# Expert layers of a two-block network on one core: both parts of x in one matmul from the first gate group on

## The chip, the core and the metric

One Trainium2 chip, one core. The time is device microseconds of one execution of the whole program. Three runs of the kernel before gave 3005.83, 3011.99 and 3014.3 us, median 3011.99.

## The reference

Two network blocks over 256 tokens of 1024 channels. The first has a convolution branch and a recurrent branch and then an expert layer; the second has two mixers, each followed by an expert layer. The change lies in the expert layer, which runs three times:

```
q = (x @ w_q) in 8 heads x 2 halves of 128;  s = q . sub_keys   (128 keys per half)
top 16 of each half, the 256 sums of pairs, top 16 of these:  expert e = i1*128 + i2
gate = softmax(the 16 best sums)                    # 128 experts per token, of 16384
act  = gelu(x . u[e]);   y = sum over the experts of gate * act * v[e]
```

## The kernel before

The kernel doesn't gather experts. It computes x . u for all 16384 experts and 256 tokens, multiplies by a dense matrix of gates that is zero almost everywhere, and multiplies that by v. A product in float32 precision is made of three matmuls: each operand is split into a high part (rounded, ScalarE, L82) and a low part (the rest, VectorE, L86), and high x high, high x low and low x high are added up.

An expert layer (`peer`) has these stages:

- Queries: 16 blocks of w_q, scores and, on VectorE, the top-16 searches.
- Up: 128 blocks of u (512 KB each, streamed by `stream`: SyncE's queue loads `raw`, four buffers; three buffers each of `hi` and `lo`). A block gives 128 experts x 256 tokens in a PSUM tile `pa`, on which ScalarE applies gelu into C (L1272, L1275).
- Down: 128 blocks of v. VectorE multiplies C by a gate tile (L1291), the result is split in two parts (L112, L113), and `acc_nat` (L168 to L170) adds up the output.

The gates of tokens 0 to 159 go through a table G in DRAM: GpSimd's indirect DMA adds them in (L1125, 128 + 32 adds a layer; `gts`, `idx` for the first 128 tokens, `pk` for the others). An add of a head waits until the adds of the head before on the same tokens have landed (`after`). At the start of the down stage GpSimd loads the first gate tile from G (L1286), behind all adds. The gates of tokens 160 to 255 are made in the core by `gates()`: 24 groups of four tokens, each with one-hot matrices B (VectorE, L1095) and A (two by VectorE, L1101, two by ScalarE, L1103 and L1104), four small matmuls (L1105), and a product into C (L1110) for the blocks done so far; for later blocks ScalarE copies the gates into C (L1109), and the block's activations are multiplied in (L1276).

The order comes from `pull`: before each block it advances the pending jobs (top-16 searches, the scatter of adds, then the spreading of picks and the groups of gates) by a budget, `rate` = 1.5, of which a group uses up 0.6 + 0.26 x 2 + 0.06 + 0.00416 x the number of blocks done. `behind` and `issue_after` keep VectorE's pieces in an order. An up block takes the form with three matmuls per 128 channels (`mm3`, 24 matmuls of 256 columns, L117 to L119) while jobs are pending, and after that the wide form: 8 matmuls of 512 columns with both parts of x (L1263), 8 of 256 columns with the low part of u (L1266), a copy (L1268) and a sum (L1270).

Of the kernel before, what the change touches and what calls it, by code (L numbers as in the profile page):

```python
# [40 lines left out]
class Net:  # L41
# [30 lines left out]
        nc.scalar.activation(warm, self.eps[RMS_EPS], AF.Sqrt)  # L72


    def stream(self, ap, n=1024):
        nc = self.nc
        raw = self.sp.tile([128, n], F32, tag="raw", name="raw", bufs=RAW)
        nc.sync.dma_start(raw, ap)
        self.chore(self.share)
        hi = self.sp.tile([128, n], F32R, tag="hi", name="hi")  # L80
        lo = self.sp.tile([128, n], F32R, tag="lo", name="lo")
        nc.scalar.copy(hi, raw)  # L82
        with self.behind():
            for i in range(0, n, 512):
                p = slice(i, min(i + 512, n))
                sub = nc.vector.tensor_tensor(lo[:, p], raw[:, p], hi[:, p].bitcast(F32), op=OP.subtract)  # L86
            self.los.append(sub)
        return hi, lo
# [966 lines left out]
    def peer(self, xh, xl, xx, wq, skT, uT, v, G, Gnext=None, rate=1.5, dve_a=2):  # L1055
# [9 lines left out]
        with ExitStack() as ctx:  # L1065
# [12 lines left out]
            cand = scr(256, 11008)  # L1078
            views = [self.topk_views(s_) for s_ in small]

            state = {"ub": 0, "tok": 256}
            SYNC = mybir.DependencyInfo(mybir.DependencyClass.Sync, mybir.DependencyReason.DATA)
            last, adds = [[], []], [[], []]

# [4 lines left out]
            def gates():  # L1089
                for t0 in range(252, TAB - 1, -4):  # L1090
                    t1 = t0 - 128
                    A = wp.tile([128, 4, 128], F32, tag="A", name="A")
                    B = wp.tile([128, 4, 128], F32, tag="B", name="B", bufs=TAIL)
                    pg = self.ps.tile([128, 4, 128], F32, tag="y", name="pg", bufs=4)
                    V.tensor_tensor(B, self.iota[:, None, :].to_broadcast([128, 4, 128]),  # L1095
                                    idT[:, 1, t1:t1 + 4, None].to_broadcast([128, 4, 128]), op=OP.is_equal)
                    for j in range(4):
                        t = t1 + j
                        i1, gg = idT[:, 0, t:t + 1], idT[:, 2, t:t + 1]
                        if j < dve_a:  # L1100
                            V.tensor_scalar(A[:, j], self.iota, i1, gg, op0=OP.is_equal, op1=OP.mult)  # L1101
                        else:
                            nc.scalar.activation(A[:, j], self.iota, AF.Abs, bias=idT[:, 3, t:t + 1])  # L1103
                            nc.scalar.activation(A[:, j], A[:, j], AF.Relu, scale=idT[:, 4, t:t + 1], bias=gg)  # L1104
                        nc.tensor.matmul(pg[:, j], B[:, j], A[:, j], start=True, stop=True)  # L1105
                    pT = pg.rearrange("p t b -> p b t")
                    n = state["ub"]
                    if n < 128:
                        nc.scalar.copy(C3[:, n:, t0:t0 + 4], pT[:, n:])  # L1109
                    V.tensor_tensor(C3[:, :n, t0:t0 + 4], C3[:, :n, t0:t0 + 4], pT[:, :n], op=OP.mult)  # L1110
                    state["tok"] = t0
                    yield 0.6 + 0.26 * dve_a + 0.06 + 0.00416 * n
# [59 lines left out]
                yield 1.8  # L1172

            def spread():
                pick = views[1]["pick"]
                pt = self.ps.tile([128, 512], F32, tag="y", name="pt", bufs=4)
                for i in range(3):
                    nc.tensor.transpose(pt[:, i * 128:i * 128 + 128], pick[:, i], self.ident)
                nc.scalar.copy(idT[:, 0:3].rearrange("p a b -> p (a b)"), pt[:, :384])
                V.tensor_scalar(idT[:, 3], idT[:, 0], -1.0, None, op0=OP.mult)  # L1180
                V.tensor_scalar(idT[:, 4], idT[:, 2], -1.0, None, op0=OP.mult)
                yield 1.0
                yield from gates()


            jobs = [[], []]
            for tt in range(2):
                for hf in range(2):
                    for g in range(8 * hf, 8 * hf + 8):
                        jobs[tt].append((g + 1, self.topk1(views[tt], S[tt], tmp, 2 * g + tt)))  # L1190
                    jobs[tt].append((8 * hf + 8, self.topk2(views[tt], cand, tmp, eq, 4 * hf)))
                    jobs[tt].append((8 * hf + 8, (scatter, scatter1)[tt](hf)))
            jobs[1].append((16, spread()))
            debt, now_ = [0.0], [None]

            def pull(budget, scored=16):


                debt[0] += budget
                with tc.issue_after(self.los[-PACE].ins):  # L1200
                    while debt[0] > 0:
                        if now_[0] is None:
                            q = next((q for q in jobs if q and q[0][0] <= scored), None)
                            if q is None:
                                debt[0] = 0.0
                                return
                            now_[0] = q.pop(0)[1]
                        c = next(now_[0], None)
                        if c is None:
                            now_[0] = None  # L1210
                        else:
                            debt[0] -= c
# [14 lines left out]
            for g in range(16):  # L1227
                hi, lo = self.stream(wq[g])
# [19 lines left out]
                self.clear(Gnext)  # L1248
                self.share = 0.35
            for b in range(128):  # L1250
                pull(rate)
                hi, lo = self.stream(uT[b])
                pa = self.ps.tile([128, 512], F32, tag="a", name="pu", bufs=4)
                src = pa
                if any(jobs) or now_[0]:
                    for c in range(8):
                        s = slice(c * 128, c * 128 + 128)
                        self.mm3(pa[:, :256], hi[:, s], lo[:, s], xh[:, c], xl[:, c], c == 0, c == 7)
                else:

                    for c in range(8):
                        s = slice(c * 128, c * 128 + 128)
                        nc.tensor.matmul(pa, hi[:, s], xx[:, c].rearrange("p x n -> p (x n)"), start=c == 0, stop=False)  # L1263
                    for c in range(8):
                        s = slice(c * 128, c * 128 + 128)
                        nc.tensor.matmul(pa[:, 256:], lo[:, s], xh[:, c], start=False, stop=c == 7)  # L1266
                    src = wp.tile([128, 256], F32, tag="sum", name="sum")
                    nc.scalar.copy(src, pa[:, 256:])  # L1268
                    with tc.issue_after(self.los[-1].ins):
                        V.tensor_tensor(src, src, pa[:, :256], op=OP.add)  # L1270
                tm = state["tok"]
                nc.scalar.activation(C3[:, b, :tm], src[:, :tm], AF.Gelu)  # L1272
                if tm < 256:
                    act = wp.tile([128, 256], F32, tag="act", name="act")
                    nc.scalar.activation(act[:, tm:], src[:, tm:256], AF.Gelu)  # L1275
                    V.tensor_tensor(C3[:, b, tm:], C3[:, b, tm:], act[:, tm:], op=OP.mult)  # L1276
                state["ub"] = b + 1
# [182 lines left out]
def build(nc, tc, a):  # L1460
    with ExitStack() as ctx:
# [16 lines left out]
        n.block1(a, *x[:2])  # L1478
        nc.gpsimd.dma_start(n.vec2, a["vec2"])
        py = peer(0, x)  # L1480
        x, y = xt(), xt()

        def first_a(fp):
            s = n.load_res(fp, hs[0])
            n.add_rms(fp, s, py, n.rows(fp, a["g_final_row"], "g"), *x[:2], norm=True)
            return s
        n.mixer_a(a, first_a, *x[:2], *y[:2], hs[1])
        py = peer(1, y)
        x, y = xt(), xt()

        def first_b(fp):
            s = n.load_res(fp, hs[1])
            n.add_ln(fp, s, py, a, (0, 1), *x[:2])
            return s
        n.mixer_b(a, first_b, *x[:2], *y[:2], hs[2])
        py = peer(2, y)
        with tc.tile_pool(name="fc", bufs=1) as fp:
            n.add_ln(fp, n.load_res(fp, hs[2]), py, a, (1, 1), dst=a["out"])
# [17 lines left out]
```

## Time and profile before

| | |
|---|---|
| profiled execution | 3022.11 us, span 3020.3 us, mean TensorE clock 0.986 |
| TensorE busy | 2929.5 us (97%) |
| VectorE busy | 2189.3 us (72%) |
| ScalarE busy | 1679.7 us (56%) |
| GpSimd busy | 947.0 us (31%) |
| L86, low parts | 1877 instructions, 1260.8 us, mean 684 ns |
| L1125, adds into G | 384 + 96 instructions, 699.7 + 150.4 us |
| matmuls of up blocks in the two forms | L117 to L119: 1656 each; L1263 and L1266: 1416 each |

Read it with the order in mind: up blocks use TensorE, VectorE and ScalarE while GpSimd's adds run beside them. The stage that follows needs both: the up blocks done and the adds landed. Three layers make every such row come three times. GpSimd's spans are rough, but their starts and the waits between them are not modelled.

### The profile page before, as it was taken

Reading aid. Unit: us, or ns where it says so; the run is one execution under the profiler, and the core shown is the slowest. Engines: PE = TensorE matmul, PEld = TensorE weight load, DVE = VectorE, ACT = ScalarE, POOL = GpSimd, SP = SyncE. Lnnn points to the kernel's source line nnn. Section 1 sums busy time; section 2 is a strip of 40 time slices with the busy share of each in tenths; the row PEclk is TensorE's granted clock in tenths of the full one; section 3 lists DMA queues with packets and bytes.
Section 4 is the critical chain, followed back from the end, with each engine's and each line's share of the span. In section 5 each row is a group of like instructions: output and inputs, shape, how many; then the busy total and the mean of one; then the engine's idle time right before and its main releaser. Section 6 shows DMA issues by size and latency. Waiting matters only on the chain.

```text
span 3020.3 us, 54408 instructions
## 1 busy us (share of the span) xinstructions
PE 2929.5 (97%) x19705; PEld 2620.8 (87%) x19705; DVE 2189.3 (72%) x5753; ACT 1679.7 (56%) x3054; POOL 947.0 (31%) x684
## 2 busy tenths in 40 slices
PE   9899999999999999999999999998999999999998
PEld 8888999987888888899998788887789998878886
DVE  6976998666666665799766666665589876666666
ACT  6345557765454454455866554445645676645543
POOL 0000387774000010058776200000008777510000
PEclk9999999999999998999999999999999999999999
DMA  9946676777677653477677676765347768767675
GB/s 310 322 128 201 175 183 161 160 190 181 224 221 225 224 191 106 151 190 188 141 179 191 188 222 225 226 219 175 108 153 194 171 145 190 189 197 223 223 225 185
DMA packets 253038, 581.46 MB, mean 193 GB/s; under 512 B 89392, under 2 KB 120384, under 8 KB 252512
## 3 DMA queue, kind: packets, MB, share of 16 engines
q1 hardware_dynamic: 172064, 535.60, 58.0%
q0 software_dynamic: 80704, 42.39, 9.2%
q8 instruction: 154, 2.52, 0.4%
q14 instruction: 116, 0.95, 0.1%
HBM read 539.78 MB, written 37.99 MB: 191 GB/s over the span
## 4 chain that ended last, share of the span: by engine, by line
PE 54%; POOL 9%; DMA 6%; issue 4%; DVE 3%; ACT 2%; POOLq 0%; DVEq 0%; SPq 0%; ACTq 0%
PE py L168 11%; PE py L170 11%; PE py L169 11%; POOL G L1125 8%; PE pu L118 3%; PE pu L117 3%; PE pu L119 3%; DMA G<-pk 3%; DMA G<-gts,idx 1%; PE pz L119 1%; PE pz L117 1%; PE pz L118 1%; DVE lo L86 1%; DMA res<-h 1%; DMA raw<-in_wq_dram 1%
## 5 line engine op out<-in xcount | busy, mean ns | idle before, releaser
L86 DVE TENSOR_TENSOR lo<-raw,hi 128x512 fp32r<-128x512 f32 (+1 forms) x1877 | 1260.8, 684 | 623.8 <-ACT hi L82 565.5
L82 ACT CAST hi<-raw 128x1024 fp32r<-128x1024 f32 (+1 forms) x939 | 980.8, 1046 | 946.0 <-issue 688.1
L1125 POOL DMA_INDIRECT G<-gts,idx x384 | 699.7, 1822 | 368.2 <-issue 133.2
L168 PE MATMUL py<-hi,cc 128*128 128x512 f32 x1536 | 600.4, 391 | 18.0 <-ACT cc L112 18.0
L170 PE MATMUL py<-hi,cc 128*128 128x512 f32 x1536 | 600.8, 391 | 0.0
L169 PE MATMUL py<-lo,cc 128*128 128x512 f32 x1536 | 600.2, 391 | 0.0
L117 PE MATMUL pu<-x,hi 128*128 128x256 f32 x1656 | 474.6, 287 | 0.0
L119 PE MATMUL pu<-x,lo 128*128 128x256 f32 x1656 | 468.7, 283 | 0.0
L118 PE MATMUL pu<-x,hi 128*128 128x256 f32 x1656 | 468.6, 283 | 0.0
L168 PEld LDWEIGHTS py<-hi,cc 128*128 128x128 f32 x1536 | 290.1, 189 | 79.7 <-ACT cc L112 19.6
L1263 PE MATMUL pu<-x,hi 128*128 128x512 f32 x1416 | 354.6, 392 | 0.0
L1286 POOL DMA_DIRECT2D gate<-G x96 | 51.9, 541 | 944.2 <-DVE C L1291 923.7
L170 PEld LDWEIGHTS py<-hi,cc 128*128 128x128 f32 x1536 | 289.7, 189 | 62.9 <-DVE cc L113 2.4
L169 PEld LDWEIGHTS py<-lo,cc 128*128 128x128 f32 x1536 | 290.0, 189 | 59.9
L118 PEld LDWEIGHTS pu<-x,hi 128*128 128x128 f32 x1656 | 317.6, 192 | 0.0
L117 PEld LDWEIGHTS pu<-x,hi 128*128 128x128 f32 x1656 | 317.4, 192 | 0.0
L119 PEld LDWEIGHTS pu<-x,lo 128*128 128x128 f32 x1656 | 317.3, 192 | 0.0
L1263 PEld LDWEIGHTS pu<-x,hi 128*128 128x128 f32 x1416 | 254.6, 189 | 45.5
L1266 PEld LDWEIGHTS pu<-x,lo 128*128 128x128 f32 x1416 | 193.2, 190 | 13.8
L1266 PE MATMUL pu<-x,lo 128*128 128x256 f32 x1416 | 197.4, 282 | 0.0
L1125 POOL DMA_INDIRECT G<-pk x96 | 150.4, 1567 | 99.6 <-DMA G<-pk 64.3
L112 ACT CAST cc<-C 128x256 fp32r<-128x256 f32 x384 | 153.0, 398 | 37.1 <-DVE C L1291 37.1
(497 smaller groups left out, 4325.1 us busy)
## 6 DMA issues: line engine op xcount, KB each, us to landing
raw<-in_u_dram SPq DMA_DIRECT2D x384, 512.0 KB
raw<-in_v_dram SPq DMA_DIRECT2D x384, 512.0 KB
G<-zero SPq DMA_DIRECT2D x120, 256.0 KB
gate<-G POOLq DMA_DIRECT2D x96, 320.0 KB
raw<-in_wq_dram SPq DMA_DIRECT2D x48, 512.0 KB
raw<-in_w_in_dram SPq DMA_DIRECT2D x38, 512.0 KB
raw<-in_a_w_inT_dram SPq DMA_DIRECT2D x14, 512.0 KB
raw<-in_b_wT_dram SPq DMA_DIRECT2D x14, 512.0 KB
```

The lines of the kernel that those rows point to most:

```text
L82: nc.scalar.copy(hi, raw)
L86: sub = nc.vector.tensor_tensor(lo[:, p], raw[:, p], hi[:, p].bitcast(F32), op=OP.subtract)
L112: nc.scalar.copy(hi, src)
L117: mm(out, lh, rh, start=start, stop=False)
L118: mm(out, lh, rl, start=False, stop=False)
L119: mm(out, ll, rh, start=False, stop=stop)
L168: mm(po[q], xh[:, ts], hi[:, h], start=f, stop=False)
L169: mm(po[q], xh[:, ts], lo[:, h], start=False, stop=False)
L170: mm(po[q], xl[:, ts], hi[:, h], start=False, stop=l)
L1125: i = nc.gpsimd.indirect_dma_start(G, bass.IndirectOffsetOnAxis(ap=ix, axis=0), g, None, compute_op=OP.add)
L1263: nc.tensor.matmul(pa, hi[:, s], xx[:, c].rearrange("p x n -> p (x n)"), start=c == 0, stop=False)
L1266: nc.tensor.matmul(pa[:, 256:], lo[:, s], xh[:, c], start=False, stop=c == 7)
```

## The change

From the moment at which the job that makes the gate groups starts (`spread`), a flag `wide` is set in this layer. From that block on, up blocks take the wide form, also while groups are pending; `pull` gets 0.55 per block instead of 1.5; and `stream` makes the low part of a u block in one VectorE instruction of 1024 columns instead of two of 512. Blocks before it, the down stage and all other streams are as they were.

```diff
-    def stream(self, ap, n=1024):
+    def stream(self, ap, n=1024, part=512):
...
-            for i in range(0, n, 512):
-                p = slice(i, min(i + 512, n))
+            for i in range(0, n, part):
+                p = slice(i, min(i + part, n))
                 sub = nc.vector.tensor_tensor(lo[:, p], raw[:, p], hi[:, p].bitcast(F32), op=OP.subtract)
...
-            state = {"ub": 0, "tok": 256}
+            state = {"ub": 0, "tok": 256, "wide": False}
...
             def spread():
+                state["wide"] = True
                 pick = views[1]["pick"]
...
-                pull(rate)
-                hi, lo = self.stream(uT[b])
+                pull(0.55 if state["wide"] else rate)
+                hi, lo = self.stream(uT[b], part=1024 if state["wide"] else 512)
...
-                if any(jobs) or now_[0]:
+                if not state["wide"]:
                     for c in range(8):
```

In the built program each layer has 69 blocks with three matmuls and 59 wide ones before, and 45 and 83 in the change. GpSimd's instructions stand in the same order in both. TensorE's order in the gate stretch, before: a group (`pg`) stands in front of nearly every block (the first matmuls of one are shown).

```order
L1105 MATMUL pg<-A,B 128x128 x4
L117 MATMUL pu<-x,hi 128x256
L118 MATMUL pu<-x,hi 128x256
L119 MATMUL pu<-x,lo 128x256
L117 MATMUL pu<-x,hi 128x256
```

In the change, the same place:

```order
L1105 MATMUL pg<-A,B 128x128 x4
L1264 MATMUL pu<-x,hi 128x512 x8
L1267 MATMUL pu<-x,lo 128x256 x8
L1264 MATMUL pu<-x,hi 128x512 x8
L1267 MATMUL pu<-x,lo 128x256 x8
L1264 MATMUL pu<-x,hi 128x512 x8
L1267 MATMUL pu<-x,lo 128x256 x8
L1105 MATMUL pg<-A,B 128x128 x4
```

Two or three wide blocks now stand between two groups. VectorE's order in the gate stretch, before (`lo` is a low part, B and A are a group's one-hot matrices, L1110 multiplies gates into C):

```order
L86 TENSOR_TENSOR lo<-raw,hi 128x512
L1110 TENSOR_TENSOR C<-C,pg 128x51x4
L86 TENSOR_TENSOR lo<-raw,hi 128x512
L1095 TENSOR_TENSOR B<-iota,idT 128x512
L1101 TENSOR_SCALAR A<-iota,idT 128x128 x2
L1276 TENSOR_TENSOR C<-C,act 128x24
```

In the change, with lines one higher behind L1175:

```order
L1095 TENSOR_TENSOR B<-iota,idT 128x512
L1110 TENSOR_TENSOR C<-C,pg 128x81x4
L1277 TENSOR_TENSOR C<-C,act 128x52
L1101 TENSOR_SCALAR A<-iota,idT 128x128 x2
L86 TENSOR_TENSOR lo<-raw,hi 128x1024
L1271 TENSOR_TENSOR sum<-sum,pu 128x256
L1277 TENSOR_TENSOR C<-C,act 128x56
L86 TENSOR_TENSOR lo<-raw,hi 128x1024
L1271 TENSOR_TENSOR sum<-sum,pu 128x256
L86 TENSOR_TENSOR lo<-raw,hi 128x1024
```

The two short low parts of a block, with other work between them, have become one long one, and sums stand between these. VectorE's order in blocks without groups, before:

```order
L86 TENSOR_TENSOR lo<-raw,hi 128x512
L1270 TENSOR_TENSOR sum<-sum,pu 128x256
L86 TENSOR_TENSOR lo<-raw,hi 128x512
L1276 TENSOR_TENSOR C<-C,act 128x96
L86 TENSOR_TENSOR lo<-raw,hi 128x512
```

And in the change:

```order
L1277 TENSOR_TENSOR C<-C,act 128x96
L1271 TENSOR_TENSOR sum<-sum,pu 128x256
L86 TENSOR_TENSOR lo<-raw,hi 128x1024
L1277 TENSOR_TENSOR C<-C,act 128x96
L1271 TENSOR_TENSOR sum<-sum,pu 128x256
```

The sum no longer stands between two halves of a low part but in front of the whole one.

## Rows read from the trace of the kernel before

**Rows 1.** Chain of waits, end of the second layer's adds: start us, us, what.

```profile
1686.29 4.93 DMA G<-pk
...
1691.97 3.18 DMA gate<-G
```

**Rows 2.** Timeline of TensorE, first down matmul of each layer: start, us; idle before.

```profile
741.36 0.79 PE L168 MATMUL py<-hi,cc 128*128 128x512 f32 x1 [5.72 <-ACT cc L112]
...
1695.99 0.79 PE L168 MATMUL py<-hi,cc 128*128 128x512 f32 x1 [5.75 <-ACT cc L112]
...
2655.43 0.79 PE L168 MATMUL py<-hi,cc 128*128 128x512 f32 x1 [6.54 <-ACT cc L112]
```

**Rows 3.** Timeline of TensorE: gate groups between three-matmul blocks; two wide blocks.

```profile
486.91 1.05 PE L1105 MATMUL pg<-A,B 128*128 128x128 f32 x8
487.72 0.36 PE L117 MATMUL pu<-x,hi 128*128 128x256 f32 x1
487.92 0.28 PE L118 MATMUL pu<-x,hi 128*128 128x256 f32 x1
...
490.68 1.06 PE L1105 MATMUL pg<-A,B 128*128 128x128 f32 x8
...
1684.49 2.00 PE L1263 MATMUL pu<-x,hi 128*128 128x512 f32 x8
...
1687.29 2.00 PE L1263 MATMUL pu<-x,hi 128*128 128x512 f32 x8
```

**Rows 4.** Windows: length, busy of each engine, clock, DMA share, GB/s.

```profile
1437.00:1525.00 88.00, 87.92 (x746) 87.70 (x746) 66.39 (x164) 70.92 (x188) 70.24 (x43) 1.00 0.65 139
1525.00:1600.00 75.00, 75.00 (x431) 65.95 (x430) 49.74 (x107) 50.59 (x108) 57.15 (x40) 1.00 0.79 190
```

**Rows 5.** Groups of adds: first row 1437 to 1525, the others 1525 to 1692.

```profile
L1125 POOL DMA_INDIRECT G<-gts,idx x43 | 70.8, 1647 | 21.9 <-issue 15.0 <-DMA G<-gts,idx 4.5 <-DVE B L1095 2.4
...
L1125 POOL DMA_INDIRECT G<-gts,idx x37 | 58.1, 1571 | 18.2 <-issue 10.7 <-DMA G<-gts,idx 7.5
L1125 POOL DMA_INDIRECT G<-pk x32 | 50.3, 1571 | 32.1 <-DMA G<-pk 20.2 <-issue 7.9 <-DMA pk<-wpk 3.9
```

**Rows 6.** Timeline of GpSimd: adds of the last five heads, second layer.

```profile
1633.04 1.75 POOL L1125 DMA_INDIRECT G<-pk  x1 [3.83 <-DMA G<-pk]
...
1669.40 1.71 POOL L1125 DMA_INDIRECT G<-pk  x1 [3.84 <-DMA G<-pk]
...
1680.54 1.74 POOL L1125 DMA_INDIRECT G<-pk  x1 [3.85 <-DMA G<-pk]
...
1684.44 1.54 POOL L1125 DMA_INDIRECT G<-pk  x1 [0.30 <-issue]
1686.29 1.57 POOL L1125 DMA_INDIRECT G<-pk  x1 [0.30 <-issue]
```

**Rows 7.** Timeline of VectorE beside them: the two low-part pieces of a block.

```profile
1679.24 0.69 DVE L86 TENSOR_TENSOR lo<-raw,hi 128x512 fp32r<-128x512 f32 x1 [0.93 <-ACT hi L82]
...
1680.17 0.68 DVE L86 TENSOR_TENSOR lo<-raw,hi 128x512 fp32r<-128x512 f32 x1
```

**Rows 8.** Timeline of VectorE: a two-operand instruction of 1024 columns.

```profile
387.62 1.22 DVE L1377 TENSOR_TENSOR C<-C 128x1024 f32<-128x1024 f32 x1
```

**Rows 9.** Timeline of GpSimd and of VectorE in the first layer's gate stretch.

```profile
497.43 2.37 POOL L1125 DMA_INDIRECT G<-gts,idx  x1 [0.30 <-issue]
...
497.09 0.68 DVE L86 TENSOR_TENSOR lo<-raw,hi 128x512 fp32r<-128x512 f32 x1
497.70 0.68 DVE L1095 TENSOR_TENSOR B<-iota,idT 128x512 f32<-128x512 f32 x1
499.31 0.60 DVE L1101 TENSOR_SCALAR A<-iota,idT 128x128 f32<-128x128 f32 x2 [0.93 <-PE pg L1105]
```

**Rows 10.** Timeline of GpSimd: waits in front of a head, gate stretch and behind it.

```profile
1470.37 1.55 POOL L1125 DMA_INDIRECT G<-gts,idx  x1 [2.43 <-DVE B L1095]
...
1538.03 1.79 POOL L1125 DMA_INDIRECT G<-gts,idx  x1 [3.74 <-DMA G<-gts,idx]
```

## The prediction

> **What bounds the kernel now.** I read the page's parts 1 and 2 first: TensorE is busy nearly everywhere, so a stage that ends earlier must show as less TensorE work or as a closed gap. Then the chain of waits: in each expert layer its stretch before the down stage does not run through TensorE but through GpSimd's scatter adds (L1125), the landing of the last head, and the gate load [rows 1]. So I went to the timeline where the down stage begins: TensorE has finished its last up block and stands still for 5.72, 5.75 and 6.54 us in the three layers until the first product with the gates is there [rows 2]. The reader is to see that up blocks and scatter adds run beside each other, that the adds end last, and that TensorE already waits for them. What ends the up stage earlier is lost; what lengthens the chain of adds by x us in each layer costs 3x. What counts then is what the change does to GpSimd.
>
> **TensorE's part.** A block that takes both parts of x in one matmul comes every 2.79 us (1687.29 - 1684.49) [rows 3]. A block in three matmuls per column group comes, with a gate group, every 3.77 us (490.68 - 486.91). The group's small matmuls take 0.81 of it (487.72 - 486.91); of the 2.96 left, the first matmul behind them takes 0.20 (to 487.92) and the 23 others 0.12 each. So a group is 0.81 + 0.08 = 0.89, and a bare block 2.88. Per layer 24 blocks change form: 24 x 0.09 = 2.1 us less. The gate groups keep their 0.89. The new gate stretch is 62 blocks and 24 groups: 62 x 2.79 + 24 x 0.89 = 194 us, against 90 us before; after it come 21 blocks without groups.
>
> Can ScalarE and VectorE follow? In the old gate stretch ScalarE is busy 70.92 of 88 us and VectorE 66.39; in the blocks without groups 50.59 and 49.74 of 75 [rows 4]. That is 3.04 and 2.84 per 3.77 us, and 1.88 and 1.85 per 2.79. A new group comes per 2.58 blocks, 8.11 us. ScalarE's work in it is between 3.04 + 1.58 x 1.88 = 6.0 and, counting one block twice, 3.04 + 2.58 x 1.88 = 7.9; VectorE's between 5.8 and 7.6. Both fit, and three buffers of high parts let ScalarE run two blocks ahead, so I cost this at nothing. Without that cover, the first 5.7 + 2.1 us in each layer would still fall into the wait before the down stage.
>
> **GpSimd's part, the one that counts.** From the first gate group to the end of the second layer there are 43 + 37 + 32 = 112 adds [rows 5]. An add that waits for nothing takes 1.54 us and the next follows 0.30 later, so the free pace is 1.85. The means are 1.647 in the old gate stretch (a pace of 1.95) and 1.571 behind it (1.87).
>
> Where does the excess come from? The add that starts at 1680.54 takes 1.74 [rows 6]; VectorE's low part (two operands in SBUF) starts at 1680.17 and ends at 1680.85 [rows 7]. If an add reads its indices 0.13 us after its start, this one waited from 1680.67 to the end of that low part, 0.18 of the 0.20 us. The same at 1669.40 and at many others; an add whose read falls on a sum from PSUM or on an idle VectorE has no excess (1684.44, 1.54). So a low part keeps an add's read out until it ends. Why is so little lost, with low parts on VectorE half of the time? Because the pieces are short: three adds (3 x 1.86 = 5.58) fit two blocks (2 x 2.79 = 5.58), the reads stand 0.93 apart within the block's period, and no piece of 0.68 is as long as that; an add that was held once falls into the gaps from then on.
>
> The piece of 1024 breaks that. Its length is not in the trace for this line; a two-operand instruction of that shape took 1.22 us [rows 8], two halves 2 x 0.68 at most. After a read that was let in when a low part ended, the next read comes 1.85 later; the next low part holds from 1.57 to 2.79. It is caught, always: any piece longer than 2.79 - 1.85 = 0.94 catches it. In blocks without groups the adds then come one per block, 2.79 instead of 1.86. A head of four adds behind a wait took 11.1 us (1680.54 - 1669.40) [rows 6]. By the phase at which its first read falls, the fourth now follows 5.6 to 6.3 us later; with the long piece three spacings of 1.85 to 2.79 and a first wait of 0 to 1.22 give 6.8 to 9.6, in the middle 8.2. So a head becomes 13.5.
>
> In the gate stretch a block takes 3.14 on average: with the low part alone caught, three adds fit two blocks, 6.28 / 3 = 2.09. The group's own two-operand instruction B (0.68) stands there too, and where it follows a low part without a gap an add waits through both: 2.37 us for the add at 497.43, with the low part from 497.09 and B to 498.38 [rows 9]. Three blocks and a group are 9.26 us; if B and A (two of 0.30) cost one of five adds there, the pace is 2.31. If all reads slipped between, it is 1.85. I take 2.17: 2.09, and 0.39 of the way (the groups per block) to 2.31.
>
> The Trainium skill (SBUF — State Buffer, Who interferes with whom) has the rule: "A DVE instruction with two SBUF inputs contends with a GpSimd instruction that reads SBUF", and who comes first holds the pair of ports for its whole instruction. The rows agree to some 0.02 us; by that rule a piece of 1024 holds as long as it runs, which is the sum below. The same section infers that descriptor generation is not held by such an instruction; that would give no change on GpSimd, and the add at 1680.54 speaks against it.
>
> **The sum, for the second layer.** The gate stretch begins about 1437 [rows 5]; the new one ends some 194 us later, about 1632, and TensorE's up work at 1695.99 - 5.75 - 2.1 = 1688 [rows 2]. Before, 20 adds (five heads, 1633.04 to 1686.29) were left at 1632, so 92 were done. Now these 92 take 43 x (2.17 - 1.95) + 49 x (2.17 - 1.87) = 24 us more, which is 2.2 heads of 11.1: 7.2 heads are left. In the 56 us to 1688 go 56 / 13.5 = 4.1. The other 3.1 run beside a VectorE that has nothing to do, at the old 11.1: 34 us, so the gate load starts at 1722 instead of 1692: 30 us later. Three layers: +91 us. The profiled execution took 3022.1 (span 3020.3 and 1.8 around it), so it would be 3113; the median of the runs shown is 3012, 0.3% below, and the forecast for it is 3012 + 91 = 3103. With 1.85 the adds would gain 5 us in the gate stretch and lose about 6 behind it: +1 a layer, 3015. With 2.09 it is +23 (3081), with 2.31 +43 (3140). The forecast's own range is 3045 to 3142.
>
> **Rivals.**
> - No change: adds aren't held by the piece of 1024 any longer than by halves, or VectorE's irregular gate groups let them slip through. Then the gate load starts where it did, TensorE's 2.1 us turn into idle time, and it stays at 3012. For: the adds in the old gate stretch, with B and A beside them, lose only 0.10 each. Against: that stretch has two blocks of 3.77 on four adds of 1.85 to 1.9, a near fit that the new one hasn't.
> - Faster: the chain's own waits get shorter. A head's wait was 2.43 us in the old gate stretch, with 139 GB/s, and 3.74 behind it, with 190 [rows 4, 10]. The new stretch moves 512 KB per 3.14 us, about 167 GB/s and the adds: by that share of the difference some four waits of 0.6 less and two of 0.7 more, 1 us a layer. Adding TensorE's end, which goes 2.1 earlier, it is at most 3 x 5: 2997 to 3009. Against: it needs the low parts to cost nothing.
> - Slower by TensorE: ScalarE issues a group's A and copies in front of a high part, and TensorE waits for that high part. If all of the 1.4 us per group were exposed, 34 us a layer; 7.8 are free, so +26 a layer, 3090. It decides from 0.33 us per group on. Against: the three buffers, and a demand that fits even when a block is counted twice.
> - That the change does nothing is excluded by the order: 83 of 128 blocks in each layer are wide in it, 59 before, and groups stand two or three blocks apart.
>
> **How the numbers follow.** Forecast 0.73, no change 0.12, faster 0.08, TensorE 0.07. A difference under 0.3% (9 us) can't be told from none here. The forecast at its lowest pace gives a little to "same": faster 0.08, same 0.14, slower 0.78. The range goes from 3010, where no change is just outside half, to 3142.
>
> **What would show it.** Right: adds in the last 20 up blocks at 2.79 us starts or with excesses near 0.9; a mean above 1.8 in the gate stretch; TensorE idle some 35 us before each down stage; more adds behind the last up block; TensorE's 24 blocks at 2.79. Wrong: adds at a mean of 1.6 or less and the gate load at its old place, or gaps on TensorE inside the gate stretch.

## The result

The change takes 3040.45 us (median of four runs, 3040.05 to 3044.54) against 3011.76: a ratio of 1.0105 [1.0081 to 1.0129], 28.7 us slower. Slower was forecast, and by the mechanism forecast, but 91 us: the size is wrong by a factor of three. 3040 lies in the wide range, 3010 to 3142, but below the forecast's own, which begins at 3045.

The profiled execution of the change has a span of 3038.8 us. What answers to [rows 1, 2] first: the chain of waits at the end of the second layer's adds (start us, us, what), then the timeline of TensorE at the first down matmul of each layer.

```profile
1697.98 1.54 POOL G L1125
...
1703.52 3.06 DMA G<-pk
...
1707.36 3.06 DMA gate<-G
```

```profile
744.30 0.80 PE L168 MATMUL py<-hi,cc 128*128 128x512 f32 x1 [11.97 <-ACT cc L112]
...
1711.26 0.80 PE L168 MATMUL py<-hi,cc 128*128 128x512 f32 x1 [21.56 <-ACT cc L112]
...
2674.90 0.80 PE L168 MATMUL py<-hi,cc 128*128 128x512 f32 x1 [14.30 <-ACT cc L112]
```

The chain is the same, and TensorE now waits 11.97, 21.56 and 14.30 us for it instead of some 6. Up to there TensorE does what was forecast. In the windows that answer to [rows 4] it is busy throughout (second layer, gate stretch, then the blocks without groups):

```profile
1440.00:1634.00 194.00, 194.00 (x1178) 172.95 (x1178) 140.21 (x277) 147.31 (x364) 151.02 (x93) 1.00 0.76 171
1634.00:1690.00 56.00, 55.70 (x324) 48.99 (x322) 32.64 (x58) 32.79 (x76) 35.73 (x20) 1.00 0.68 180
```

ScalarE is busy 147 of the 194 us (76%) and VectorE 140 (72%), near the lower ends of what was worked out (6.0 to 7.9 and 5.8 to 7.6 of 8.11 us). Now GpSimd beside VectorE in the third layer's blocks without groups, as in [rows 6, 7]:

```profile
2638.57 2.49 POOL L1125 DMA_INDIRECT G<-pk  x1 [0.30 <-issue]
2641.37 2.49 POOL L1125 DMA_INDIRECT G<-pk  x1 [0.30 <-issue]
2644.16 2.49 POOL L1125 DMA_INDIRECT G<-pk  x1 [0.30 <-issue]
```

```profile
2638.42 1.23 DVE L86 TENSOR_TENSOR lo<-raw,hi 128x1024 fp32r<-128x1024 f32 x1 [1.07 <-ACT hi L82]
2639.56 0.25 DVE L1277 TENSOR_TENSOR C<-C,act 128x96 f32<-128x96 f32 x1
2639.73 0.42 DVE L1271 TENSOR_TENSOR sum<-sum,pu 128x256 f32<-128x256 f32 x1
2641.21 1.22 DVE L86 TENSOR_TENSOR lo<-raw,hi 128x1024 fp32r<-128x1024 f32 x1 [1.06 <-ACT hi L82]
```

One add per block, 2.79 apart. The add that starts at 2638.57 would read its indices at 2638.70, 0.13 behind its start as the prediction takes it; the low part holds from 2638.42 to 2639.65, so it waits 0.95, and 1.54 + 0.95 = 2.49. The next read falls 0.29 behind the start of the next low part, and so on: each add is caught, as worked out.

In the gate stretch it is otherwise. Groups of adds, the counterpart of [rows 5]; the first two rows are from 1440 to 1634, the third from 1634 to 1690:

```profile
L1125 POOL DMA_INDIRECT G<-gts,idx x79 | 134.3, 1700 | 37.1 <-issue 28.9 <-DVE C L1277 4.4 <-DMA G<-gts,idx 3.8
L1125 POOL DMA_INDIRECT G<-pk x10 | 16.3, 1634 | 6.0 <-DMA G<-pk 3.2 <-issue 2.7
...
L1125 POOL DMA_INDIRECT G<-pk x16 | 34.4, 2150 | 20.6 <-DMA G<-pk 13.4 <-DMA pk<-wpk 3.9 <-issue 3.3
```

The means are 1.70 and 1.63: a pace of 2.00, where 2.17 was taken. Two timelines show why, VectorE's low parts and GpSimd's adds in one cycle of three blocks and a group:

```profile
1527.33 1.23 DVE L86 TENSOR_TENSOR lo<-raw,hi 128x1024 fp32r<-128x1024 f32 x1 [0.43 <-ACT hi L82]
...
1530.44 1.23 DVE L86 TENSOR_TENSOR lo<-raw,hi 128x1024 fp32r<-128x1024 f32 x1 [0.73 <-ACT hi L82]
...
1532.91 1.23 DVE L86 TENSOR_TENSOR lo<-raw,hi 128x1024 fp32r<-128x1024 f32 x1 [0.91 <-ACT hi L82]
...
1534.50 0.68 DVE L1095 TENSOR_TENSOR B<-iota,idT 128x512 f32<-128x512 f32 x1
...
1536.61 1.23 DVE L86 TENSOR_TENSOR lo<-raw,hi 128x1024 fp32r<-128x1024 f32 x1 [0.41 <-ACT hi L82]
```

```profile
1526.59 1.55 POOL L1125 DMA_INDIRECT G<-gts,idx  x1 [0.30 <-issue]
1528.44 1.55 POOL L1125 DMA_INDIRECT G<-gts,idx  x1 [0.30 <-issue]
1530.30 1.55 POOL L1125 DMA_INDIRECT G<-gts,idx  x1 [0.30 <-issue]
1532.16 1.55 POOL L1125 DMA_INDIRECT G<-gts,idx  x1 [0.30 <-issue]
1534.01 1.55 POOL L1125 DMA_INDIRECT G<-gts,idx  x1 [0.30 <-issue]
1535.87 1.55 POOL L1125 DMA_INDIRECT G<-gts,idx  x1 [0.30 <-issue]
```

The low parts stand 3.11, 2.47 and 3.70 apart. Together that is 9.28, and five adds of 1.856 are 9.28 as well. Reads at 1528.57, 1530.43, 1532.29, 1534.14 and 1536.00 fall on no low part and not on B, two of them by 0.01 us. So it goes on until a wait for a head's landing breaks the fit; then, as a rule, two or three adds are caught, and the next fit again. 65 of the 89 adds of this stretch take less than 1.6 us.

### The profile page after: what moved, and what is told of

Read it like the earlier page. It is cut to its first block, busy times and chain, and to the rows that moved or that the text cites. A ratio compares the mean times of both kernels' runs of the same rounds, so it can differ in the third digit from the quotient of the medians.

```text
span 3038.8 us, 53298 instructions
## 1 busy us (share of the span) xinstructions
PE 2925.5 (96%) x19129; PEld 2593.1 (85%) x19129; DVE 2190.6 (72%) x5573; ACT 1682.5 (55%) x3123; POOL 975.4 (32%) x684
## 4 chain that ended last, share of the span: by engine, by line
PE 53%; POOL 9%; DMA 6%; issue 3%; DVE 3%; ACT 1%; POOLq 0%; DVEq 0%; ACTq 0%; SPq 0%
PE py L168 11%; PE py L170 11%; PE py L169 11%; POOL G L1125 9%; PE pu L119 3%; PE pu L118 3%; PE pu L117 3%; DMA G<-pk 3%; DMA G<-gts,idx 2%; PE pu L1264 1%; PE pz L117 1%; PE pz L119 1%; PE pz L118 1%; DVE lo L86 1%; PE pu L1267 1%
## 5 line engine op out<-in xcount | busy, mean ns | idle before, releaser
L86 DVE TENSOR_TENSOR lo<-raw,hi 128x512 fp32r<-128x512 f32 (+2 forms) x1628 | 1228.6, 767 | 622.2 <-ACT hi L82 619.5
L168 PE MATMUL py<-hi,cc 128*128 128x512 f32 x1536 | 600.4, 391 | 47.8 <-ACT cc L112 47.8
L1264 PE MATMUL pu<-x,hi 128*128 128x512 f32 x1992 | 505.5, 395 | 0.0
L1264 PEld LDWEIGHTS pu<-x,hi 128*128 128x128 f32 x1992 | 357.6, 189 | 64.0
L118 PE MATMUL pu<-x,hi 128*128 128x256 f32 x1080 | 305.9, 283 | 0.0
L117 PE MATMUL pu<-x,hi 128*128 128x256 f32 x1080 | 305.9, 283 | 0.0
L119 PE MATMUL pu<-x,lo 128*128 128x256 f32 x1080 | 305.6, 283 | 0.0
L1267 PEld LDWEIGHTS pu<-x,lo 128*128 128x128 f32 x1992 | 271.6, 190 | 20.2
L1267 PE MATMUL pu<-x,lo 128*128 128x256 f32 x1992 | 277.5, 282 | 0.0
L1125 POOL DMA_INDIRECT G<-pk x96 | 180.5, 1880 | 86.0 <-DMA G<-pk 50.6
L118 PEld LDWEIGHTS pu<-x,hi 128*128 128x128 f32 x1080 | 207.3, 192 | 0.0
L119 PEld LDWEIGHTS pu<-x,lo 128*128 128x128 f32 x1080 | 207.3, 192 | 0.0
L117 PEld LDWEIGHTS pu<-x,hi 128*128 128x128 f32 x1080 | 207.3, 192 | 0.0
## 6 DMA issues: line engine op xcount, KB each, us to landing
G<-zero SPq DMA_DIRECT2D x120, 256.0 KB
```

Source lines behind the costliest of these rows:

```text
L117: mm(out, lh, rh, start=start, stop=False)
L118: mm(out, lh, rl, start=False, stop=False)
L119: mm(out, ll, rh, start=False, stop=stop)
L168: mm(po[q], xh[:, ts], hi[:, h], start=f, stop=False)
L1125: i = nc.gpsimd.indirect_dma_start(G, bass.IndirectOffsetOnAxis(ap=ix, axis=0), g, None, compute_op=OP.add)
```

## The experiments

Each ratio is to runs of the kernel before on the same chip. Theory A: an add's read waits for the end of a low part on which it falls, and the chain of adds sets the start of the down stage. B: the uneven places of groups and the wide form hold the adds. C: TensorE is fed worse in the gate stretch.

**The low part in two again** (the rest of the change stays):

```diff
-                hi, lo = self.stream(uT[b], part=1024 if state["wide"] else 512)
+                hi, lo = self.stream(uT[b], part=512)
```

> The change with the low part of a u block in two instructions of 512 again; wide form and spread groups stay. Theory A (an add's read is caught by a low part longer than 0.94 us, and the chain of adds sets the start of the down stage): adds in the last 20 up blocks go back to starts 1.86 apart, the chain behind the 48th add loses the 13 to 17 us per layer that it gained, time 2995 to 3015, and TensorE's wait before the down stage falls to 8 us or less. Rival B (the groups' uneven places and the wide form beside them hold the adds, the length of the low part doesn't matter): 3035 to 3045, adds still 2.79 apart. Rival C (TensorE is fed worse in the gate stretch): 3035 to 3045 with gaps on TensorE.

3002.07 us, ratio 0.9990 [0.9975 to 1.0006]: the whole loss is gone. In the first layer the stretch behind the 48th add lost 6 us and not the 17 expected (table below); the 49th add still stands in the top-16 stage there and takes 8.71 us (start 457.13). The adds in the last blocks are 1.85 apart:

```profile
2602.36 1.54 POOL L1125 DMA_INDIRECT G<-pk  x1 [4.08 <-DMA G<-pk]
2604.21 1.54 POOL L1125 DMA_INDIRECT G<-pk  x1 [0.30 <-issue]
2606.06 1.54 POOL L1125 DMA_INDIRECT G<-pk  x1 [0.30 <-issue]
```

B and C fall: wide form and spread groups stand unchanged in this kernel.

**The long low part alone**, in the kernel before (`stream` with `part` as in the change):

```diff
-                hi, lo = self.stream(uT[b])
+                hi, lo = self.stream(uT[b], part=512 if any(jobs) or now_[0] else 1024)
```

> The kernel before with one thing of the change alone: the low part in one instruction of 1024 in the 59 blocks that are wide there already; groups one per block as before. Theory A: all 69 adds beside these blocks are caught, one per block of 2.79 us; 69 x 0.93 = 64 us more per layer until the up blocks end, of which what is left over runs at 1.85 behind them: heads of 13.5 to 14.5 instead of 11.1, gate load 25 to 40 us later per layer, time 3085 to 3130, worse than the whole change. Rival B: 3012, as before.

3106.56 us, ratio 1.0324 [1.0302 to 1.0347], over three times the loss of the whole change. From GpSimd's timeline, third layer:

```profile
2604.52 2.49 POOL L1125 DMA_INDIRECT G<-gts,idx  x1 [0.30 <-issue]
2607.31 2.49 POOL L1125 DMA_INDIRECT G<-gts,idx  x1 [0.30 <-issue]
2610.11 2.49 POOL L1125 DMA_INDIRECT G<-gts,idx  x1 [0.31 <-issue]
```

**The change with groups as dense as before:**

```diff
-                pull(0.55 if state["wide"] else rate)
+                pull(rate)
```

> The change with the budget of 1.5 per block kept, so that the groups stand one per block again and are over after 24 blocks; wide form and low part of 1024 stay. Theory A, with what the runs so far showed (adds slip between low parts that a group sets 2.5 to 3.7 us apart, and are caught one per block where low parts stand 2.79 apart): only 24 blocks are like that instead of 62, 59 have low parts 2.79 apart, so it comes near the run with the long low part alone, 3080 to 3110. If spreading the groups is itself what costs: under 3030.

3108.4 us, ratio 1.0327 [1.0296 to 1.0357]. So spreading the groups isn't what costs; beside the long low part it takes away two thirds of the loss, since it leaves 21 instead of 59 blocks in which low parts stand 2.79 apart.

**Pieces of 640 and 384, and of 896 and 128** (`part=640` and `part=896` in place of 1024):

> The change with the low part cut into 640 and 384. The long piece takes about 0.15 + 640/960 = 0.82 us, below 0.94. Theory A: like two pieces of 512, adds in the last 20 blocks 1.86 apart, time within 8 us of the run with 512. A theory by which any longer piece costs in proportion: a quarter of the way from the run with 512 to the change.

3008.2 us, ratio 1.0013 [0.9994 to 1.0031], like two halves.

> The change with the low part cut into 896 and 128. The long piece takes about 1.08 us, above 0.94. Theory A: adds in the last 20 blocks mostly 2.79 apart, as in the change, time 3030 to 3045. A theory by which the number of instructions counts (two instead of one): like the run with 512.

3009.73 us, ratio 1.0021 [1.0006 to 1.0037]: a miss. Adds are caught, but few. Its timelines of VectorE and of GpSimd show the reason:

```profile
2601.78 1.09 DVE L86 TENSOR_TENSOR lo<-raw,hi 128x896 fp32r<-128x896 f32 x1 [0.68 <-PE pu L1267]
...
2604.26 1.09 DVE L86 TENSOR_TENSOR lo<-raw,hi 128x896 fp32r<-128x896 f32 x1 [0.85 <-ACT hi L82]
...
2607.37 1.09 DVE L86 TENSOR_TENSOR lo<-raw,hi 128x896 fp32r<-128x896 f32 x1 [0.68 <-ACT hi L82]
```

```profile
2605.41 1.54 POOL L1125 DMA_INDIRECT G<-pk  x1 [2.38 <-DMA G<-pk]
2607.26 1.54 POOL L1125 DMA_INDIRECT G<-pk  x1 [0.30 <-issue]
2609.11 1.54 POOL L1125 DMA_INDIRECT G<-pk  x1 [0.31 <-issue]
```

With the second piece VectorE's order became another: the long pieces stand 2.48 and 3.11 apart. Behind the one that ends at 2605.35 no long piece stands until 2607.37, 2.02, more than an add's 1.85; so two reads fit there and three in two blocks. The bound of 0.94 holds only for low parts that stand evenly. With one long piece in each block, three adds get into two blocks only where two reads fall into one gap between long pieces, so where that gap is over 1.85: 2.79 - 1.23 = 1.56 in the change isn't. This reading was made behind the run, and no further run put it to the test.

**Without the last 16 adds of a layer**, in the kernel before and in the change (the gates of heads 4 to 7 of tokens 128 to 159 are missing in the output):

```diff
-                for h in range(4 * hf, 4 * hf + 4):
+                for h in range(0, 4 * (1 - hf)):
```

> The kernel before without the last 16 of the 160 adds of each layer (heads 4 to 7 of tokens 128 to 159 left out of the table). The chain of adds ends some 45 us earlier, before the up blocks. Theory A: TensorE's wait before the down stage falls from 6 us to what one block needs (1 to 3 us), time 9 to 18 us under the kernel before. If the adds aren't what the down stage waits for: no difference.

> The change without the same 16 adds per layer. The four heads left out took 50 us or more here. Theory A: the loss of the change is gone, and TensorE's 2.1 us per layer show: 3 to 10 us under the kernel before without these adds. Rival C (TensorE is fed worse in the gate stretch): above it.

2992.56 us, ratio 0.9950 [0.9935 to 0.9965], and 2989.72, ratio 0.9942 [0.9924 to 0.9959]. Without the end of the chain the change isn't slower, and the first down matmul follows the last up block; in the first layer of the shortened kernel before:

```profile
735.00 1.12 PE L1266 MATMUL pu<-x,lo 128*128 128x256 f32 x8
735.96 0.40 PE L168 MATMUL py<-hi,cc 128*128 128x512 f32 x1
```

TensorE's gain of 6 us by the wide form is 2.8 here, just under the 3 to 10 expected and within what such runs differ by. The two traces have it: the first down matmul comes 384.4, 383.0 and 383.0 us after the first add of its layer in the one, and 382.1, 380.9 and 380.7 in the other, 2.1 to 2.3 less per layer, where 2.1 was worked out.

**A version meant to beat both.** In the top-16 stage of the kernel before an add waits far longer. Timelines of GpSimd and, behind the dots, of VectorE, first layer:

```profile
381.98 10.09 POOL L1125 DMA_INDIRECT G<-gts,idx  x1 [0.30 <-issue]
...
388.76 1.29 DVE L86 TENSOR_TENSOR lo<-raw,hi 128x512 fp32r<-128x512 f32 x2
389.96 0.68 DVE L1377 TENSOR_TENSOR C<-C 128x512 f32<-128x512 f32 x1
390.56 0.21 DVE L1383 TENSOR_REDUCE C<-C 128x4 f32<-128x64 f32 x1
```

That add ends at 392.07; less the 1.41 behind a read, it was let in at 390.66. That is when the first instruction with a single operand ran; from its read at 382.11 on, 8.6 us, there had been only instructions with two. So such instructions were put in, on top of the change with two halves:

```diff
+            if j % 2 == 1:
+                V.memset(self.nap, 0.0)
             if j % 4 == 3:
```

> A version meant to beat both: the change with the low part in two pieces of 512, and in the top-16 stage a memset of one column behind every second of the 16 one-hot sums of VectorE (L1372), an instruction without SBUF operands to read, at which a waiting add gets in. In the kernel before single adds wait there for up to 10 us, some 20 to 28 us per layer. Theory A: the first 48 adds take 100 to 115 us instead of 112 to 130, the chain ends before the up blocks, and TensorE's wait falls to that of the kernels without the last adds: 2985 to 2998. If an add isn't let in by such an instruction: like the run with 512, 3002.

2985.07 us, ratio 0.9929 [0.9911 to 0.9946]: faster than both, and the longest of the first 48 adds takes 3.35 us instead of up to 10.83. That an add gets in at the memset itself is not shown. Only one add that had waited was let in at one (459.96, a memset at 459.89). Others beside the memsets got in between two instructions with two operands, as here, VectorE and then GpSimd, first layer (line numbers are one higher and more in this kernel):

```profile
377.75 0.68 DVE L87 TENSOR_TENSOR lo<-raw,hi 128x512 fp32r<-128x512 f32 x1
377.78 0.06 DVE L1377 MEMSET nap<- 128x1 f32 x1
378.36 0.68 DVE L87 TENSOR_TENSOR lo<-raw,hi 128x512 fp32r<-128x512 f32 x1
...
378.13 1.73 POOL L1126 DMA_INDIRECT G<-gts,idx  x1 [0.30 <-issue]
```

This add was let in at 378.45, at the end of the first piece, though the next stood right behind it. How the memsets bring that about is open. The same memsets in the kernel before, and in the change with its long low part:

> The kernel before with the one-column memsets in the top-16 stage and nothing else. Theory A: the chain of adds gets some 20 us shorter per layer and ends before the up blocks, so the down stage starts behind TensorE as in the kernel before without its last adds: 2988 to 2996, and 3 x 2.1 = 6 us above the version with wide form, spread groups and two pieces. If the gain of that version came from its up blocks and not from the adds: 3002 or more.

> The change (low part of 1024) with the same memsets. Theory A: the first 48 adds take some 105 us, the others 269 to 273 as in the change, together 375 to 380 instead of the 386 of the kernel before; the up blocks' end is at about 384: close to or just behind TensorE, 2988 to 3002. If the long low part costs also beside TensorE's own work: over 3010.

2994.23, ratio 0.9934 [0.9914 to 0.9954], and 2994.65, ratio 0.9941 [0.9920 to 0.9961]. The 6 us expected between the two versions without long low parts don't show in the ratios, 0.9934 and 0.9929, on two chips; in their traces up blocks end 2.3 to 2.7 us earlier per layer in the one with the wide form. The stretches of the chain, from the starts of the first add, of the 49th and of the gate load in each layer, in us:

| | first 48 adds | the others | TensorE's waits for the gates, sum |
|---|---|---|---|
| before | 130.4, 129.3, 129.5 | 255.7, 255.5, 256.0 | 18.0 |
| the change | 117.4, 129.5, 121.9 | 272.7, 269.0, 269.2 | 47.8 |
| change, two halves | 111.9, 122.5, 129.2 | 266.3, 253.8, 249.5 | 6.3 |
| change, 640 and 384 | 128.6, 124.4, 129.3 | 251.8, 254.2, 253.7 | 11.5 |
| change, 896 and 128 | 117.3, 129.5, 130.1 | 260.3, 256.4, 255.5 | 19.7 |
| before, long low part | 117.4, 132.2, 129.0 | 292.2, 285.5, 286.2 | 104.4 |
| change, dense groups | 117.1, 129.5, 128.9 | 294.0, 293.7, 291.2 | 122.0 |
| memsets, two halves | 108.3, 106.7, 107.6 | 258.4, 252.5, 257.3 | none |
| memsets, before | 109.2, 107.9, 108.2 | 259.7, 256.8, 257.0 | none |
| memsets, change | 109.0, 108.1, 110.3 | 273.4, 268.5, 267.9 | 7.1 |

The last column follows from the sum of the other two. Up blocks end 383 to 384 us after the first add with the form of the kernel before, and 380 to 382 with the wide one; from the start of the gate load to the first down matmul it is 4 us. What the sum and these 4 us are over the up blocks' end is waited for, and in some layers up to 3.4 us are waited for without it.

## Why the prediction was wrong

- The bound was right: the chain of adds sets the start of the down stage. Shortened, it gives 15.6 us (3008.13 to 2992.56); lengthened by 13 to 17 us a layer, it costs.
- TensorE's part was right: the gate stretch takes 194 us without a gap, and ScalarE and VectorE follow.
- The hold by a low part was right: in the kernel before with the long low part, 95% of the 169 adds behind the 48th whose read, taken 0.13 us after the start, falls on a low part take what the prediction's rule gives, to 0.03 us. Right was with it the 2.79 per add in the blocks without groups. A head there takes 14.6 us (1674.06 to 1688.69), 13.5 were taken:

```profile
1674.06 1.68 POOL L1125 DMA_INDIRECT G<-pk  x1 [3.90 <-DMA G<-pk]
...
1688.69 1.54 POOL L1125 DMA_INDIRECT G<-pk  x1 [4.56 <-DMA G<-pk]
```

- The step that failed is the pace in the gate stretch: "I take 2.17". Measured: 2.00, a mean of 1.70 for 79 adds and 1.63 for ten, plus 0.30. The working spread the low parts evenly over 3.14 us and added the group's B as one more obstacle. They stand 3.11, 2.47 and 3.70 apart, five adds fit the cycle, and the rival's argument (adds slip through) is right for this stretch, for most of its adds. With 2.00 the sum of the prediction reads: 92 adds lose 43 x 0.05 + 49 x 0.13 = 8.5 us, 0.8 heads; 5.8 are left, 56 / 14.6 = 3.8 run beside the up blocks, two run behind them at 9.3 (1688.69 to 1697.98): a gate load at 1706.6, where 1707.36 was measured. That is 14.6 us later than before instead of 30, +44 us for three layers: 3056 instead of 3103.
- These 44 us are what the profiles show for the 112 adds of each layer, all three layers together. What adds take above 1.54 us grows from 19 to 73 us; their waits between heads and the last landing fall from 131 to 121. So the rival "faster" had its shorter waits, 10 us in all, against 54 of longer adds.
- Part of the 44 us is not seen in the time: the first 48 adds took 13, 0 and 8 us less in the change's profile. In the first and third layers no instruction of that stretch differs, in the second only its last 7 us have long low parts; and it takes 112 to 132 us in all kernels without memsets, depending on how many single adds take up to 10.8 us. So it doesn't look like the change's doing; why an add gets stuck in one execution and not in another was not tried. The prediction took this stretch as fixed. For the same reason the two profiles can't settle the last of the 28.7 us: they differ by 18.5, and the profiled execution of the kernel before, 3022.11, is slower than all four timed ones (3005.83 to 3014.3). How long the first 48 adds took in those isn't on record.
- Of the other rivals, B and "no change" fell with the run of the long low part alone; C (the prediction's "slower by TensorE") with the change in two halves and with TensorE busy for 194.00 of 194 us.
- Of the signs named, two came (adds 2.79 apart in the last blocks; 3, 7 and 4 adds behind the up blocks' end, none before) and two did not: the mean in the gate stretch is 1.70 and not above 1.8, and TensorE waits 12 to 22 us and not some 35.

## What to carry to other kernels

An engine off the critical path may still set a stage's end through a third one: fusing two VectorE instructions into one saved VectorE time that nobody needed and cost each of GpSimd's adds that it caught up to 0.95 us. When two engines share something that one holds for whole instructions, lay their periods side by side: here it counted whether the gaps between long holds let the other's next piece in, not how much was held in all. Where the other must get in, try a tiny instruction in between: 96 memsets of 59 ns were worth 18.6 us in the kernel before.

## What the runs showed of the hardware that was not expected

- GpSimd's indirect adds and VectorE's instructions with two SBUF operands can run in step: in blocks without groups adds lose only 0.03 us each (1.571 against 1.54, [rows 5]) beside two low parts of 0.68 in 2.79 us, half of VectorE's time. Beside one low part of 1.23 us the places decide: 2.79 apart it costs an add 0.95, and 3.11, 2.47 and 3.70 apart it costs five adds in step with it next to nothing.
- Behind each other, without a gap, such instructions can keep an add out for 8.55 us (the add of 10.09 us above), over 21 of them, although between other pairs it got in at once (1.74 for the add at 1680.54, [rows 6]). Which of the two happens was not settled.
- The longer wait costs the work behind it no more of TensorE's clock than the shorter one did. In the first 4 us from the first down matmul the granted clock is 0.50 of full speed, so 1.2 of 2.4 GHz, after waits of 6 us in the kernel before and of 12 and 22 us in the change, and 0.53 after the wait of 14; in the 4 us behind it the mean is 0.95, 0.81 and 0.85 before and 0.77, 0.90 and 1.00 in the change. The first down matmuls take 0.63 us instead of 0.39 in both. The windows of the second layer, first before and then in the change, show it:

```profile
1696.00:1700.00 4.00, 4.00 (x9) 2.88 (x10) 3.83 (x10) 2.74 (x8) 0.00 (x0) 0.50 0.34 86
1700.00:1704.00 4.00, 4.00 (x15) 3.19 (x15) 2.19 (x7) 1.46 (x2) 0.00 (x0) 0.81 0.48 180
...
1711.50:1715.50 4.00, 4.00 (x10) 2.76 (x11) 3.83 (x12) 2.53 (x7) 0.00 (x0) 0.50 0.35 90
1715.50:1720.00 4.50, 4.50 (x20) 3.69 (x19) 2.47 (x7) 2.09 (x4) 0.43 (x1) 0.93 0.51 153
```

The columns are the window, its length, and then busy time of PE, PEld, VectorE, ScalarE and GpSimd with their instructions, the granted clock, the share of the DMA engines and GB/s: the clock column is to be read, 0.50 and then 0.81 before, 0.50 and then 0.93 in the change.
